# A hybrid encoder layer in float32: later attention pairs read behind a marker, biases one tile ahead, attention and decay started some units later

## The chip, the cores and the metric

The kernel runs on one core of a Trainium2 chip. The metric is the device time of one execution in microseconds (us): 2143.28 is the median of three runs of the kernel before, which lie between 2139.96 and 2145.53. Times inside an execution come from one profiled execution, counted from the start of its span.

A core has engines that run side by side: TensorE (PE; its weight loads are PEld), VectorE (DVE), ScalarE (ACT), GpSimd (POOL) and SyncE (SP). Each works off its own list of instructions strictly in order. An instruction that waits holds up all that stand behind it on its engine. Transfers are started by SP (queue q1 in the profile) and by POOL (queue q0), and all run on the same 16 DMA engines.

## The reference

One encoder layer on a sequence of 1024 tokens with width 1024, all in float32:

```
x = LN1(alpha*x + 0.5*SwiGLU_1(x))
x = LN2(alpha*x + W_out(sig(g_na)*P_na(NA(x)) + sig(g_gla)*P_gla(GLA(x))))
x = LN3(alpha*x + 0.5*SwiGLU_2(x))
```

NA is neighbourhood attention with 8 heads of width 64 on a grid of 16 rows x 64 columns. Each token looks at a window of 8 x 16 tokens; a bias for each offset is added to the scores before the softmax. GLA is gated linear attention with 4 heads, chunked, one scan in each direction, whose decay gates come from a low-rank product. One input projection makes all queries, keys, values and gates of both.

## The kernel before, in words

Every float32 factor is split into a high and a low part (ACT copies the high part, DVE subtracts for the low one), and each product is three matmuls: high x high, high x low, low x high. Three such matmuls of 128 x 512 are one **step**.

The program has stages: the first feed-forward block; the input projection; a stage in which attention runs between dense steps; a GLA stage in the same manner; merging, output projection and norm; the second feed-forward block. The change touches the attention stage and the GLA stage.

**The order on PE is written out by hand.** `run` works through streams of dense steps and adds 0.65 units to a clock for each step. `at(delay, f)` puts a piece of work on a list, and `run` emits it once that clock has passed its time. So a unit is a place in the stream of dense steps, not a time. On the other engines a scheduler places instructions by priority; `hoist()` raises that priority.

**Attention stage.** The dense stream is `tok_major` for the GLA values (8 tiles of 8 steps, lines 871 to 873), then four gate products (lines 122 to 124): 128 steps. Each finished tile of `tok_major` leaves PSUM by an ACT copy into one of two stage buffers (`sl`, line 876) and is stored by SP (`gv<-sl`, line 877). The third copy needs the first store to have landed.

Between these steps run 64 attention tiles, i = 0 to 63. Tile i belongs to head pair i // 16 and to head i % 2 of it; each pair has two blocks of query rows, and each of these four blocks of columns. `na_events` spreads them: event s does the values of tile s-3 (`po`, only for odd tiles), the transposes of tile s-2 (`pt`) and the scores of tile s (`s`). A tile's chain is: scores on PE (lines 1047, 1049), bias added and the minimum taken on DVE (`e`, line 1053), exponential on ACT (line 1055), reciprocal and product on DVE (1057, 1058), three transposes on PE (line 1066), copy on ACT (1069), values on PE (line 1084).

What a head pair needs is read back from DRAM by `qk_pair`: on POOL's queue eight pieces of queries (`q`), four of keys (`k`) and one of the keys' low parts (`kl`); on SP's queue 16 small transfers of values (`vp`, line 1023), whose packets are 512 bytes. All these buffers exist twice. The bias of a tile (`bt`, line 1039) is read by SP when its scores are emitted, at tiles 0, 2, 6, 8, 10, 14 and so on; two tiles share one load and the two middle column blocks too. `bt` has two buffers.

**GLA stage.** `gate_na` streams 8 x 24 dense steps; `gla_decay` of a head begins with two matmuls on the decay ranks (`zs`, line 1172), which need `dlT`, made by ACT and DVE (lines 1150 to 1152) from a small read (`dlr`). `gate_na` frees PSUM with a sigmoid on ACT (line 1296).

Of the kernel before, what the change touches and what calls it, by code (L numbers as in the profile page):

```python
# [8 lines left out]
F32 = mybir.dt.float32  # L9
F32R = mybir.dt.float32r  # L10
BF16 = mybir.dt.bfloat16
U32 = mybir.dt.uint32
AF = mybir.ActivationFunctionType
# [5 lines left out]
P = 128  # L19
# [3 lines left out]
HF = 512  # L23
# [12 lines left out]
NEG = -1.0e30  # L36
HOIST = 100
WARM = 30
GLA_D0 = 6.0
GLA_T0 = 27.0  # L40
GLA_DT = 31.0
GLA_NEXT = 8.5
GLA_OUT = (15.0, 28.8, 28.8, 36.0)
NA_T0 = 13.0
NA_DT = 1.05
NA_GATES = (4, 5, 6, 7)
GLA_GATES = (1, 2, 3)
FIRST = (1, 2, 4, 8)
# [13 lines left out]
COLW = (24, 32, 32, 24)  # L62
BOFF = (0, 288, 288, 672)
# [4 lines left out]
def hybrid_layer(ctx, tc, xT, wg1, wu1, wds1, wd1, wg2, wu2, wds2, wd2, wcol, wnv, wgv, wdl, wgate,  # L68
                 wbr, wout, lnp, bias, dec2, bdec, ng, ident_d, masks_d, ln3, outN):
    nc = tc.nc  # L70
# [4 lines left out]
    def pool(stack, name, bufs=1, space=None):  # L75
        kw = dict(name=name, bufs=bufs)
        if space is not None:
            kw["space"] = space
        if space is not DRAM:
            kw["reuse_waits"] = "tile"  # L80
        return stack.enter_context(tc.tile_pool(**kw))
# [13 lines left out]
    def nm(s):  # L95
        uid[0] += 1
        return f"{s}_{uid[0]}"
# [86 lines left out]
    def at(delay, fn):  # L184
        uid[0] += 1
        pending.append((clock[0] + delay, uid[0], fn))
        pending.sort(key=lambda e: e[:2])

    def run(*streams):
        for st_ in streams:  # L190
            for cost in st_:
                clock[0] += cost
                while pending and pending[0][0] <= clock[0]:
                    pending.pop(0)[2]()
# [6 lines left out]
    def hoist():  # L201
        return tc.high_priority(offset=HOIST)
# [652 lines left out]
    def tok_major(w_d, dst, alloc=None, wq=None):  # L855
        wq = wq or tok_weights(w_d, 4 if alloc is None else 2)
        for i in range(len(wq) // 2, 4):
            raw = wpool.tile([P, D], F32, tag="raw", name=nm("raw"), bufs=2)
            with tc.high_priority(offset=HOIST):
                nc.sync.dma_start(raw, w_d[i])  # L860
                for o in (0, HF):
                    wq.append(alloc())
                    split(raw[:, o:o + HF], *wq[-1])
        for t in range(8):
            h, c = t // 4, (t % 4) * P
            ps = dps()
            for k in range(KD):
                xh, xl = x1[k][h]
                wh, wl = wq[k]
                a, b = xh[:, c:c + P], xl[:, c:c + P]  # L870
                nc.tensor.matmul(ps, a, wh, start=k == 0, stop=False)  # L871
                nc.tensor.matmul(ps, a, wl, start=False, stop=False)
                nc.tensor.matmul(ps, b, wh, start=False, stop=k == KD - 1)  # L873
                yield STEP
            sb = stage()
            nc.scalar.activation(sb, ps, AF.Copy)
            nc.sync.dma_start(dst(t), sb)
# [117 lines left out]
    npool = pool(nap, "npool")  # L995
# [1 line left out]
    grid = lambda t: t.rearrange("p (r c) -> p r c", c=64)  # L997
    pair = {}

    def qk_pair(p):  # L1000
        k2 = [npool.tile([P, S], F32R, tag="k2", name=nm("k2"), bufs=4) for _ in range(2)]
        kl = npool.tile([P, S], F32R, tag="kl", name=nm("kl"), bufs=2)
        vp = npool.tile([P, 16, P], F32, tag="vp", name=nm("vp"), bufs=2)
        q2 = [[None, None], [None, None]]
        pair[p] = (q2, k2, kl, vp)
        load = lambda dst, src: nc.gpsimd.dma_start(dst.bitcast(F32), src)
        for h in range(2):
            hs = slice(h * HF, (h + 1) * HF)
            for hh in range(2):
                a, o = slice(64 * hh, 64 * hh + 64), slice(64 - 64 * hh, 128 - 64 * hh)  # L1010
                t = npool.tile([P, HF], F32R, tag="q2", name=nm("q2"), bufs=8)
                q2[hh][h] = t
                load(t[a], qks[p, 0, a, hs])
                load(t[o], qks[p, 1, a, hs])
                if h == 0:
                    load(k2[hh][a], qks[p, 2, a])
                    load(k2[hh][o], qks[p, 2, a])
            if h == 0:
                load(kl, qks[p, 3])
        for b in range(4):  # L1020
            w = COLW[b]
            for g in range(4):
                nc.sync.dma_start(vp[:4 * w, 4 * b + g, :],  # L1023
                                  vgrid[4 * g:4 * g + 4, COL0[b]:COL0[b] + w, p * P:(p + 1) * P])


    na_e, na_t, na_b, na_o = {}, {}, {}, {}

    def na_idx(i):
        return i // 16, (i // 8) % 2, i % 2, (i // 2) % 4  # L1030

    def na_scores(i):
        p, rb, hh, b = na_idx(i)
        q2, k2, kl, vp = pair[p]
        w, c0 = COLW[b], COL0[b]
        nk = 12 * w
        if hh == 0 and b != 2:
            bt = npool.tile([P, 2, 384], F32, tag="bt", name=nm("bt"), bufs=2)
            nc.sync.dma_start(bt[:, :, :nk], bias[p, rb, :, 2 * BOFF[b]:2 * BOFF[b] + 2 * nk]
                              .rearrange("q (h k) -> q h k", h=2))  # L1040
            na_b[0] = bt
        bt = na_b[0]
        a = slice(64 * hh, 64 * hh + 64)
        ka = (slice(4 * rb, 4 * rb + 12), slice(c0, c0 + w))
        qa = slice(P * b, P * b + P)
        s = aux.tile([P, 384], F32, tag="s", name=nm("s"), bufs=2)
        nc.tensor.matmul(s[:, :nk], q2[hh][rb][:, qa], grid(k2[hh])[:, ka[0], ka[1]],
                         start=True, stop=False)
        nc.tensor.matmul(s[:, :nk], q2[hh][rb][a, qa], grid(kl)[a, ka[0], ka[1]],  # L1049
                         start=False, stop=True)  # L1050
        e = npool.tile([P, 384], F32, tag="e", name=nm("e"), bufs=3)
        sm = npool.tile([P, 4], F32, tag="sm", name=nm("sm"), bufs=4)
        nc.vector.tensor_tensor_reduce(e[:, :nk], s[:, :nk], bt[:, hh, :nk], -1.0,
                                       3.0e38, ALU.add, ALU.min, sm[:, 0:1])
        nc.scalar.activation(e[:, :nk], e[:, :nk], AF.Exp, bias=sm[:, 0:1], scale=-1.0,
                             accum_out=sm[:, 1:2])
        nc.vector.reciprocal(sm[:, 2:3], sm[:, 1:2])
        nc.vector.tensor_scalar(e[:, :nk], e[:, :nk], sm[:, 2:3], None, ALU.mult)
        na_e[i] = e

    def na_transpose(i):
        w = COLW[(i // 2) % 4]
        e = na_e.pop(i)
        pt = aux.tile([P, 384], F32, tag="pt", name=nm("pt"), bufs=1)
        for g in range(3):
            nc.tensor.transpose(pt[:4 * w, g * P:(g + 1) * P], e[:, 4 * w * g:4 * w * (g + 1)],  # L1066
                                ident)
        et = npool.tile([P, 384], F32, tag="et", name=nm("et"), bufs=3)
        nc.scalar.activation(et[:4 * w], pt[:4 * w], AF.Copy)
        na_t[i] = et  # L1070
# [21 lines left out]
    def na_events(s0, s1, t0, t1):  # L1092
        u = (t1 - t0) / (s1 - s0)
        for s in range(s0, s1):
            t = t0 + (s - s0) * u
            if s >= 3:
                at(t, lambda i=s - 3: na_values(i))
            if 2 <= s < 66:
                at(t, lambda i=s - 2: na_transpose(i))
            if s < 64:  # L1100
                at(t, lambda i=s: na_scores(i))

    def gate_gla(j):
        w = load_w(wgate[KD + j], D)
        for h in range(2):
# [3 lines left out]
            nc.scalar.activation(sb, ps, AF.Copy)  # L1109
            nc.sync.dma_start(gts[j, :, h * HF:(h + 1) * HF], sb)  # L1110

    qk_pair(0)
    for p in range(1, 4):
        at(NA_T0 + (16 * p - 13) * NA_DT, lambda p=p: qk_pair(p))
    na_events(0, 67, NA_T0, NA_T0 + 67 * NA_DT)
    run(tok_major(wgv, lambda t: gv[t], wq=wq), *[gate_gla(j) for j in NA_GATES])
    flush()
# [171 lines left out]
    def gate_na(j):  # L1289
        wga = load_w(wgate[j], D)  # L1290
        wb = load_w(wbr[0, j], HF)
        for h in range(2):
            pg = dps()
            yield from mm_steps(pg, wga, x1h[h])
            sb = gp.tile([P, HF], F32, tag="m1", name=nm("m1"), bufs=2)
            nc.scalar.activation(sb, pg, AF.Sigmoid)  # L1296
            py = dps()
            yield from mm_steps(py, wb, [o_na[k][h] for k in range(4)])
            nc.vector.tensor_tensor(sb, sb, py, ALU.mult)
            nc.sync.dma_start(m1s[j, :, h * HF:(h + 1) * HF], sb)  # L1300
# [9 lines left out]

    at(GLA_D0, lambda: gla_decay(0))
    for hd in range(4):
        b = GLA_T0 + GLA_DT * hd
        add = lambda t, f, *a: at(b + t, lambda: f(*a))
# [6 lines left out]
        if hd < 3:  # L1321
            add(GLA_NEXT, gla_decay, hd + 1)
        for i, t in enumerate(GLA_OUT):
            add(t, (gla_out, gla_otrans)[i % 2], hd, i // 2)
# [164 lines left out]
```

## Time and profile before

| what | value |
|---|---|
| median of three runs | 2143.28 us |
| the profiled execution | 2146.0 us, its span 2144.1 us |
| mean granted PE clock | 0.987 |
| PE busy in the span | 2081.7 us (97%) |
| DVE, ACT, POOL busy | 1379.6, 894.3, 156.9 us |
| attention stage, first dense step to the last `po` | 875.1 to 1093.9 us |
| first `zs` of the GLA stage | 1105.1 us |

The span and the profiled execution differ by 1.9 us, which lie outside the span. The profile attributes idle time of an engine to the instruction that released it. Busy time of a group, means and counts are given by line and by tile name with the buffer's number left out, so `bt` is any bias tile.

### The profile page before, as it was taken

What the parts mean: (1) busy time and instruction counts of PE and PEld (TensorE: products, weight loads), DVE (VectorE), ACT (ScalarE), POOL (GpSimd) and SP (SyncE); (2) the same over time, 40 slices, a digit from 0 to 9 for tenths busy, and PEclk for the clock granted to TensorE, in tenths of its full rate; (3) what the DMA queues carried; (4) which work ended last, traced back from release to release, by engine and by line L of the source; (5) the groups of instructions that cost most, each with busy time, mean ns of one, the idle gap of its engine ahead of it and who ended that gap; (6) DMA issues with size and microseconds to landing.
All of it is one profiled execution on the core that took longest, in us unless ns stands there. A gap on an engine that the chain in (4) does not pass through costs nothing.

```text
span 2144.1 us, 26681 instructions
## 1 busy us (share of the span) xinstructions
PE 2081.7 (97%) x9722; PEld 1693.5 (79%) x9722; DVE 1379.6 (64%) x2356; ACT 894.3 (42%) x1500; POOL 156.9 (7%) x204
## 2 busy tenths in 40 slices
PE   9999999999999999679999999999999999999997
PEld 7888888888887788556667888877888888888887
DVE  8667776466678854035447674788876777547647
ACT  6444444312225543135555553445544444322212
POOL 0000000000015021311010000034000000000001
PEclk9999999999999999889999999999999999999999
DMA  4434443496520343646333433622243443386732
GB/s 150 152 133 152 172 148 125 157 334 216 192 88 30 121 164 111 165 125 195 95 107 104 129 109 121 199 96 69 85 173 135 151 174 128 125 295 222 242 108 79
DMA packets 156164, 315.07 MB, mean 147 GB/s; under 512 B 17312, under 2 KB 41632, under 8 KB 156032
## 3 DMA queue, kind: packets, MB, share of 16 engines
q1 hardware_dynamic: 146880, 283.99, 39.4%
q0 software_dynamic: 9152, 29.37, 4.8%
q8 instruction: 77, 1.26, 0.2%
q14 instruction: 55, 0.45, 0.1%
HBM read 216.16 MB, written 97.12 MB: 146 GB/s over the span
## 4 chain that ended last, share of the span: by engine, by line
PE 87%; DVE 6%; SPq 2%; ACT 2%; DMA 1%; issue 1%; POOL 1%; DVEq 0%; ACTq 0%; POOLq 0%
PE d L559 18%; PE d L561 18%; PE d L560 18%; PE d L122 5%; PE d L124 5%; PE d L123 5%; PE d L661 3%; PE d L659 3%; PE d L660 3%; SPq L1023 2%; PE pt L1066 1%; PE po L1084 1%; PE d L871 1%; PE s L1049 1%; PE d L873 1%
## 5 line engine op out<-in xcount | busy, mean ns | idle before, releaser
L131 ACT ACTIVATE wh<-raw 128x512 fp32r<-128x512 f32 (+4 forms) x148 | 111.6, 763 | 194.7 <-PE d L560 86.3
L132 DVE TENSOR_TENSOR wl<-raw,wh 128x512 fp32r<-128x512 f32 (+4 forms) x148 | 125.2, 854 | 101.9 <-ACT wh L131 101.6
L122 PE MATMUL d<-xh,wh 128*128 128x512 f32 x384 | 158.6, 413 | 3.9 <-ACT m L1296 3.5
L681 DVE TENSOR_TENSOR a<-a,d 128x512 f32<-128x512 f32 (+1 forms) x152 | 99.9, 657 | 92.0 <-PE d L561 60.6
L559 PE MATMUL d<-a,wh 128*128 128x512 f32 x384 | 149.8, 390 | 2.4 <-DVE hr L587 1.6
L123 PE MATMUL d<-xl,wh 128*128 128x512 f32 x384 | 150.7, 393 | 1.0 <-POOL xl L412 0.5
L124 PE MATMUL d<-xh,wl 128*128 128x512 f32 x384 | 150.9, 393 | 0.5 <-DVE wl L112 0.5
L561 PE MATMUL d<-xh,wl 128*128 128x512 f32 x384 | 149.5, 389 | 0.5 <-DVE wl L132 0.5
L559 PE MATMUL d<-xh,wh 128*128 128x512 f32 x384 | 149.5, 389 | 0.0
L560 PE MATMUL d<-a,wh 128*128 128x512 f32 x384 | 149.4, 389 | 0.0
L560 PE MATMUL d<-xl,wh 128*128 128x512 f32 x384 | 149.4, 389 | 0.0
L561 PE MATMUL d<-a,wl 128*128 128x512 f32 x384 | 149.4, 389 | 0.0
L559 PE MATMUL d<-hh,hh 128*128 128x512 f32 x384 | 149.4, 389 | 0.0
L560 PE MATMUL d<-hl,hh 128*128 128x512 f32 x384 | 149.4, 389 | 0.0
L561 PE MATMUL d<-hh,hl 128*128 128x512 f32 x384 | 149.4, 389 | 0.0
L131 ACT ACTIVATE hh<-sr 128x512 fp32r<-128x512 f32 x168 | 105.9, 631 | 87.0 <-DVE sr L500 25.1
L659 PE MATMUL d<-hh,wh 128*128 128x512 f32 (+1 forms) x368 | 134.3, 365 | 0.0
L661 PE MATMUL d<-hh,wl 128*128 128x512 f32 (+1 forms) x368 | 133.0, 362 | 0.0
L660 PE MATMUL d<-hl,wh 128*128 128x512 f32 (+1 forms) x368 | 133.0, 361 | 0.0
L112 DVE TENSOR_TENSOR wl<-raw,wh 128x512 fp32r<-128x512 f32 (+1 forms) x77 | 78.0, 1013 | 60.2 <-ACT wh L111 55.4
L132 DVE TENSOR_TENSOR hl<-sr,hh 128x512 fp32r<-128x512 f32 x168 | 114.4, 695 | 1.8 <-ACT hh L131 1.0
L111 ACT ACTIVATE wh<-raw 128x512 fp32r<-128x512 f32 (+1 forms) x77 | 67.6, 878 | 111.2 <-PE d L123 48.9
(330 smaller groups left out, 4909.7 us busy)
## 6 DMA issues: line engine op xcount, KB each, us to landing
raw<-in_wu SPq DMA_DIRECT2D x44, 512.0 KB
raw<-in_wg SPq DMA_DIRECT2D x43, 512.0 KB
ops<-oh SPq DMA_DIRECT2D x84, 256.0 KB
ops<-ol SPq DMA_DIRECT2D x84, 256.0 KB
oh<-ops SPq DMA_DIRECT2D x48, 256.0 KB
ol<-ops SPq DMA_DIRECT2D x48, 256.0 KB
hid<-oh SPq DMA_DIRECT2D x40, 256.0 KB
hid<-ol SPq DMA_DIRECT2D x40, 256.0 KB
```

The lines of the kernel that those rows point to most:

```text
L122: nc.tensor.matmul(ps, a, xh, start=k == 0, stop=False)
L123: nc.tensor.matmul(ps, a, xl, start=False, stop=False)
L124: nc.tensor.matmul(ps, wl[:, k * m:(k + 1) * m], xh, start=False, stop=k == n - 1)
L131: nc.scalar.activation(hi, src, AF.Copy)
L132: nc.vector.tensor_tensor(lo, src, hi.bitcast(F32), ALU.subtract)
L559: nc.tensor.matmul(ps, a, xh, start=first and k == 0, stop=False, **sg)
L560: nc.tensor.matmul(ps, a, xl, start=False, stop=False, **sg)
L561: nc.tensor.matmul(ps, wl[:, k * P:(k + 1) * P], xh, start=False, stop=k == n - 1, **sg)
L659: nc.tensor.matmul(ps, wh, hi, start=k == 0, stop=False)
L660: nc.tensor.matmul(ps, wh, lo, start=False, stop=False)
L661: nc.tensor.matmul(ps, wl, hi, start=False, stop=k == n - 1)
L681: nc.vector.tensor_tensor(a, a, ps, ALU.add)
```

## The change

Five edits:

- `qk_pair` of pairs 1 to 3 gets a marker: one column of the small softmax tile `sm` of the attention tile emitted last. Before any read, POOL copies that column into the first column of each of the seven q, k and kl tiles and into `vp`. The reads write over these cells, so none of the pair's reads, on POOL's queue or on SP's, can begin before DVE has worked on that tile. The call moves from 3 to 5.5 events after the pair before begins (tiles 5, 21 and 37).
- The bias of tile 0 is read ahead of `qk_pair(0)`; every other bias is read when the bias tile before it is taken into use.
- The attention events begin at 20 units instead of 13, and are 0.94 instead of 1.05 units apart.
- In the GLA stage the first decay comes at 8.5 instead of 6 units, the heads at 29.5 + 30.3 per head instead of 27 + 31, and the outputs slightly sooner after them.
- The sigmoid in `gate_na` is hoisted.

```diff
-GLA_D0 = 6.0
-GLA_T0 = 27.0
-GLA_DT = 31.0
+GLA_D0 = 8.5
+GLA_T0 = 29.5
+GLA_DT = 30.3
-GLA_OUT = (15.0, 28.8, 28.8, 36.0)
-NA_T0 = 13.0
-NA_DT = 1.05
+GLA_OUT = (15.0, 28.3, 28.3, 35.5)
+NA_T0 = 20.0
+NA_DT = 0.94
...
-    def qk_pair(p):
+    def qk_pair(p, mark=None):
...
+            for hh in range(2):
+                q2[hh][h] = npool.tile([P, HF], F32R, tag="q2", name=nm("q2"), bufs=8)
+        if mark is not None:
+            m = mark[:, 0:1]
+            for t in (*k2, kl, *q2[0], *q2[1]):
+                nc.gpsimd.tensor_copy(t[:, 0:1], m)
+            nc.gpsimd.tensor_copy(vp[:, :, 0:1], m.unsqueeze(2).to_broadcast([P, 16, 1]))
...
+    def bias_tile(i):
+        p, rb, _, b = na_idx(i)
+        nk = 12 * COLW[b]
+        bt = npool.tile([P, 2, 384], F32, tag="bt", name=nm("bt"), bufs=2)
+        nc.sync.dma_start(bt[:, :, :nk], bias[p, rb, :, 2 * BOFF[b]:2 * BOFF[b] + 2 * nk]
+                          .rearrange("q (h k) -> q h k", h=2))
+        na_b["next"] = bt
...
         if hh == 0 and b != 2:
-            bt = npool.tile([P, 2, 384], F32, tag="bt", name=nm("bt"), bufs=2)
-            nc.sync.dma_start(bt[:, :, :nk], bias[p, rb, :, 2 * BOFF[b]:2 * BOFF[b] + 2 * nk]
-                              .rearrange("q (h k) -> q h k", h=2))
-            na_b[0] = bt
+            na_b[0] = na_b.pop("next")
+            if i < 62:
+                bias_tile(i + (2 if b != 1 else 4))
...
         na_e[i] = e
+        na_mark[0] = sm
...
+    bias_tile(0)
     qk_pair(0)
     for p in range(1, 4):
-        at(NA_T0 + (16 * p - 13) * NA_DT, lambda p=p: qk_pair(p))
+        at(NA_T0 + (16 * p - 10.5) * NA_DT, lambda p=p: qk_pair(p, na_mark[0]))
...
-            nc.scalar.activation(sb, pg, AF.Sigmoid)
+            with hoist():
+                nc.scalar.activation(sb, pg, AF.Sigmoid)
```

**SP at the start of the attention stage.** Before, the list reads (values of pair 0, two stores, biases of tiles 0 and 2, values of pair 1):

```order
L110 DMA raw_8497<-in_wgate 128x1024
L1023 DMA vp_7357<-vscr 96x1x128 x4
L1023 DMA vp_7357<-vscr 128x1x128 x8
L1023 DMA vp_7357<-vscr 96x1x128 x4
L877 DMA gv<-sl_7416 128x512
L877 DMA gv<-sl_7444 128x512
L1039 DMA bt_7463<-in_bias 128x2x288
L1039 DMA bt_7498<-in_bias 128x768
L1023 DMA vp_7519<-vscr 96x1x128 x4
```

With the change (the biases are those of tiles 0, 2, 6, 8, then the values of pair 1, then the biases of tiles 10 and 14):

```order
L1043 DMA bt_7354<-in_bias 128x2x288
L1030 DMA vp_7359<-vscr 96x1x128 x4
...
L877 DMA gv<-sl_7418 128x512
L877 DMA gv<-sl_7446 128x512
L1043 DMA bt_7499<-in_bias 128x768
...
L1043 DMA bt_7676<-in_bias 128x2x288
L1030 DMA vp_7619<-vscr 96x1x128 x4
L1030 DMA vp_7619<-vscr 128x1x128 x8
L1030 DMA vp_7619<-vscr 96x1x128 x4
L877 DMA gv<-sl_7687 128x512
L1043 DMA bt_7727<-in_bias 128x768
L1043 DMA bt_7778<-in_bias 128x2x288
```

The first bias has moved ahead of the 16 value reads of pair 0. The first stores and the bias of tile 2 are still behind them. The bias of tile 10 stands behind the 16 value reads of pair 1, which now wait for POOL's copies. In the same way the biases of tiles 26 and 42 stand directly behind the value reads of pairs 2 and 3.

**ACT at the start of the attention stage.** Before (`sl` is the copy of a finished `tok_major` tile, `e` the exponential of tiles 0 and 1):

```order
L876 ACTIVATE sl_7416<-d_7391 128x512
L876 ACTIVATE sl_7444<-d_7419 128x512
L1055 ACT_TABLE_LOAD
L1055 ACTIVATE e_7468,sm_7469<-e_7468,sm_7469 128x288
L1055 ACTIVATE e_7480,sm_7481<-e_7480,sm_7481 128x288
L876 ACTIVATE sl_7509<-d_7447 128x512
```

With the change:

```order
L876 ACTIVATE sl_7418<-d_7393 128x512
L876 ACTIVATE sl_7446<-d_7421 128x512
L876 ACTIVATE sl_7474<-d_7449 128x512
L1069 ACT_TABLE_LOAD
L1069 ACTIVATE e_7504,sm_7505<-e_7504,sm_7505 128x288
L876 ACTIVATE sl_7513<-d_7477 128x512
```

The third copy, which needs the first store's buffer back, now stands ahead of the first exponential. On PE the first scores follow 31 dense steps instead of 21.

**ACT at the start of the GLA stage**, with the change (`m` is the sigmoid's tile; before, all four `dlT` copies stood ahead of the table load):

```order
L1166 ACTIVATE dlT<-dlr_9266 32x512
L1313 ACT_TABLE_LOAD
L1313 ACTIVATE m_2179_9313<-d_9288 128x512
L1167 ACTIVATE dlT<-dlr_9266 32x512
L1166 ACTIVATE dlT<-dlr_9271 32x512
L1167 ACTIVATE dlT<-dlr_9271 32x512
```

The sigmoid with its table load has moved between the copies that `zs` needs. On PE the first `zs` follows 142 dense steps of the two stages instead of 138.

More of the change, by code (lines that the diff above doesn't have):

```diff
@@ L1007, in qk_pair @@
         for h in range(2):
+            for hh in range(2):
[5 more added lines that the diff above has]
+            nc.gpsimd.tensor_copy(vp[:, :, 0:1], m.unsqueeze(2).to_broadcast([P, 16, 1]))
+        for h in range(2):
             hs = slice(h * HF, (h + 1) * HF)
@@ L1010, in qk_pair @@
                 a, o = slice(64 * hh, 64 * hh + 64), slice(64 - 64 * hh, 128 - 64 * hh)
-                t = npool.tile([P, HF], F32R, tag="q2", name=nm("q2"), bufs=8)
-                q2[hh][h] = t
+                t = q2[hh][h]
                 load(t[a], qks[p, 0, a, hs])
@@ L1024, in qk_pair @@
                                   vgrid[4 * g:4 * g + 4, COL0[b]:COL0[b] + w, p * P:(p + 1) * P])
-    na_e, na_t, na_b, na_o = {}, {}, {}, {}
+    na_e, na_t, na_b, na_o, na_mark = {}, {}, {}, {}, {}
     def na_idx(i):
         return i // 16, (i // 8) % 2, i % 2, (i // 2) % 4
+    def bias_tile(i):
[5 more added lines that the diff above has]
+        na_b["next"] = bt
     def na_scores(i):
```

## The prediction

> **What bounds the kernel now.** I read the page's first line, then the list of waits between 840 and 1130 us for PE and DVE (columns: time in total, times, longest), since PE is busy 97% of the span and the change touches only this part.
>
> ```profile
> span 2144.1 us, 26681 instructions
> ...
> PE pt L1066 <- DVE e L1058: 22.0, 1, 22.0
> PE s L1049 <- DMA kl<-qks: 5.4, 1, 5.4
> PE zs L1172 <- DVE dlT L1152: 4.2, 2, 3.5
> ...
> DVE e L1053 <- DMA bt<-in_bias: 44.8, 2, 43.6
> ```
>
> PE stands still twice at the first attention tiles, 5.4 us for the keys' low part and 22.0 us at the first transpose. The second is the bias: DVE waited 43.6 us for it in one go. The view by stretches (length, then busy time of PE, PEld, DVE, ACT, POOL, then granted clock) shows what follows a stall:
>
> ```profile
> 896.00:901.00 5.00, 4.81 (x11) 2.91 (x10) 0.00 (x0) 0.00 (x0) 3.22 (x7) 0.55 0.85 197
> 923.00:932.00 9.00, 9.00 (x35) 6.00 (x34) 2.48 (x9) 2.54 (x7) 0.00 (x0) 0.54 0.39 112
> 1107.00:1113.00 6.00, 6.00 (x17) 4.71 (x16) 1.88 (x2) 4.76 (x7) 0.35 (x1) 0.57 0.30 94
> ```
>
> After each stall PE runs at little over half clock: 4.81 x 0.45 = 2.2, 9.0 x 0.46 = 4.1 and 6.0 x 0.43 = 2.6 us lost, 3.0 us a stall on average. The Trainium skill (TensorE: Matmul & The Clock Gate, Part 1: The HAM clock gate) puts the slow time at some 3.4 us of sustained work; the trace shows 5 to 9 us, and by the page each stall below would cost 1.7 us instead of 3.0.
>
> So the first tiles lose 5.4 + 22.0 + 2.2 + 4.1 = **33.7 us**, which is all this part of the change can give back. Why the bias is late is in SP's own list (start, duration, instruction):
>
> ```profile
> 877.82 37.31 SPq L1023 DMA_DIRECT2D vp<-vscr  x16
> 915.24 0.88 SPq L877 DMA_DIRECT2D gv<-sl  x2
> 916.21 0.94 SPq L1039 DMA_DIRECT2D bt<-in_bias  x2
> ...
> 968.76 10.73 SPq L1023 DMA_DIRECT2D vp<-vscr  x16
> ```
>
> The bias stands behind 16 value reads, which hold SP 37.31 us here and 10.73 us in the third group. What differs is POOL's queue q0, in the views of the transfers (packets, MB, share of the DMA engines) of 880.4 to 893.4, of 910 to 912.5 and of 971 to 979 us:
>
> ```profile
> q0 software_dynamic: 831, 2.61, 95.1%
> q1 hardware_dynamic: 334, 0.23, 7.7%
> ...
> q0 software_dynamic: 39, 0.10, 12.4%
> ...
> q1 hardware_dynamic: 1362, 0.71, 31.4%
> ```
>
> While POOL's reads run, SP's queue moves 0.23 MB in 13 us; without them 0.71 MB in 8 us. POOL's last reads run out by 912.5 us, and SP is free at 915.2. SP's transfers do not share, they wait until POOL's are through. This row decides the case.
>
> **The change part by part.** The sum goes against the profiled execution's 2146.0 us; the median of the runs is 2.7 us lower.
>
> *First tiles.* The rows of PE, ACT and DVE that I use:
>
> ```profile
> 875.12 0.39 PE L871 MATMUL d<-wh,xh 128*128 128x512 f32 x1
> ...
> 875.80 0.39 PE L871 MATMUL d<-wh,xh 128*128 128x512 f32 x1
> ...
> 889.40 0.29 PE L1047 MATMUL s<-k,q 128*128 128x288 f32 x1
> 895.12 0.60 PE L1049 MATMUL s<-kl,q 64*128 64x288 f32 x1 [5.42 <-DMA kl<-qks]
> ...
> 922.80 0.87 PE L1066 MATMUL pt<-ident,e 128*96 128x128 f32 x3 [21.99 <-DVE e L1058]
> ...
> 886.20 0.60 ACT L876 ACTIVATE sl<-d 128x512 f32<-128x512 f32 x1 [4.84 <-PE d L873]
> 886.82 1.28 ACT L1055 ACT_TABLE_LOAD   x1
> 921.52 0.54 ACT L1055 ACTIVATE e<-e,sm 128x288 f32<-128x288 f32 x1 [33.42 <-DVE sm L1053]
> ...
> 921.02 0.46 DVE L1053 CUSTOM_DVE_ANT_0 e<-s,bt 128x288 f32<-128x288 f32 x1 [43.60 <-DMA bt<-in_bias]
> ```
>
> A dense step takes 0.68 us. The first scores stand 10 steps later, at 889.4 + 6.8 = 896.2 us, after the 895.1 at which the keys have landed: the 5.4 us are gone. The first bias, now ahead of the values, has 0.29 MB and lands before that or about then. But PE reaches the first transpose 3 steps and two score pairs of 0.63 us on, at 899.5, and there ACT is late: its third copy stands ahead of the first exponential and needs the first `gv` store to have landed, which SP still starts behind the 16 value reads. Pair 0's reads on POOL end at about 893.4: the transfers of 876 to 916 us list, for two pairs,
>
> ```profile
> q<-qks POOLq DMA_DIRECT2D x16, 128.0 KB, 9.0
> k<-qks POOLq DMA_DIRECT2D x8, 256.0 KB, 10.0
> kl<-qks POOLq DMA_DIRECT2D x2, 512.0 KB, 11.6
> ```
>
> or 2.6 MB a pair, and the row of 880.4 to 893.4 has 2.61. The last value read leaves SP some time later: bounds are 3.2 us (before: from about 912 to 915.2) and 10.7 (nothing issued ahead). I take 8, as the bias is ahead. The store goes at 901.9 and takes 4 us (bounds 2 and the 4.8 us from the bias's issue at 916.21 to DVE at 921.02). So ACT goes on at 905.9, and with copy 0.60, table load 1.28 and the 1.28 from the exponential's start to the transpose (921.52 to 922.80) PE goes on at 909.0. Stall **9.5 us** (bounds 2.7 and 13.0), with the clock 12.5. The bias of tile 2 hides in it.
>
> *The marker.* Eight small POOL copies a pair. The nearest rows:
>
> ```profile
> 1088.73 0.10 POOL L1136 MEMSET rmask<- 128x8 f32 x1
> ...
> 1087.52 0.95 POOL L1135 MEMSET rmask<- 128x1024 f32 x1 [79.66 <-PE s L1047]
> ```
>
> So 0.8 to 7.6 us for eight; they are one column wide, I take 1.6. The copies cost no busy engine anything. What they release is the point: POOL's 2.62 MB and SP's 16 value reads now start together, after tiles 5, 21 and 37, and behind the value reads SP holds the bias of tiles 10, 26 and 42, five tiles on. In the profile the second and third groups of values started when POOL's reads were through. Now it is as at 877.8 us:
>
> ```profile
> 877.65 1.06 POOL L1006 DMA_DIRECT2D q<-qks  x2
> ```
>
> From this issue to the end of that pair's reads at 893.4 are 15.7 us. Then 6 us until SP has issued the last value read (bounds 3.2 and 10.7; no bias is ahead here), 0.9 for the store and the bias (0.88 for two in the row), 4.8 to landing: **27.4 us** after the copies. With 1.6 for the copies and 1.8 from DVE's start to the transpose (921.02 to 922.80), the transposes of tile 10 can run 30.8 us after DVE has done tile 5. PE gets there earlier. Between lie 10 steps, six score pairs, six groups of transposes and four of values, whose lengths I take from
>
> ```profile
> 1084.29 0.88 PE L1084 MATMUL po<-et,vp 128*64 128x128 f32 x12
> 1085.10 0.55 PE L1066 MATMUL pt<-ident,e 128*128 128x128 f32 x3
> 1085.40 0.38 PE L1047 MATMUL s<-k,q 128*128 128x288 f32 x1
> ...
> 1086.03 0.50 PE L122 MATMUL d<-xh,wh 128*128 128x512 f32 x1
> ```
>
> by their starts: 0.81 + 0.1 for values, 0.30 transposes, 0.63 to 0.72 scores, 0.68 + 0.1 a step after scores: 3.6 + 1.8 + 4.0 + 7.5 = 16.9, less 0.6 for DVE's pass, 16.3 us of cover. Stall 30.8 - 16.3 = **14.5 us**, with the clock 17.5, and the same for pairs 2 and 3, whose lists differ little: 52.5. Bounds: with no hold-up at all SP needs 10.73 + 0.9 + 4.8 = 16.4 us and the stall is 3.5; with the mean of 37.31 and 10.73 for the 16 reads (half of POOL's traffic) it is 24.0 + 5.7 = 29.7 and 16.8.
>
> *Spacing.* 0.94 against 1.05 units changes which steps lie between, not their number; PE does the same work. Cost nothing.
>
> *GLA.* `zs` comes four steps later, 2.7 us, but the hoisted sigmoid with its table load (1.28 + 0.60) now stands between the copies it waits for. Of 4.2 us, 3.4 stay, and the clock loss too. The sigmoids themselves are awaited by PE in
>
> ```profile
> PE d L122 <- ACT m L1296: 3.5, 3, 1.2
> ```
>
> of which hoisting may take all or, with more table loads, nothing; I take 1.5. Together **-2.3 us**, between -10.3 (4.2, 2.6 and 3.5 all gone) and +4 (the decay chain late by two table loads and reaching its transposes).
>
> Sum: -33.7 + 12.5 + 52.5 - 2.3 = +29.0, or 2175.0 for the profiled execution; against the median, 2143.3 + 29.0 = 2172.3.
>
> **The rivals.**
>
> *Both queues get their turn (faster).* The place is the DMA engines while POOL reads pairs 1 to 3. If SP's small packets are served alongside, the 16 reads need about the 10.73 us of the quiet case, the first store lands in time, and the three stalls are 3.5 us: -33.7 + 3 x (3.5 + 2) - 2.3 = -19.5, some 2124; with a landing in under 2 us nothing stalls and it is 2107. It decides once SP needs under some 14 us for the 16 reads. For it speaks the 10.73 us of the third group, whose first reads still met POOL's last; against it 7.7% to 95.1% above. The Trainium skill says this would be the rule (DMA: Bandwidth & Descriptors, Queues, rings and completion order): each DMA engine goes round its queues packet by packet. The transfers of 880.4 to 893.4 us do not agree, 334 packets against 831 with SP's list full. By the page it is the faster rival that holds.
>
> *Part of the hold-up (no change).* If POOL's reads take 10 us, because no weights are read beside them, and SP has issued more ahead, the bias lands after 20 us: stalls of 7.1 + 3, and 6 + 3 at the first transpose: -33.7 + 9 + 30.3 - 2.3 = +3.3, some 2147.
>
> *The marker does not hold the reads back.* Then the pairs collide as before. POOL's copies stand ahead of the reads in its list and SP's value reads wait for POOL, so I give this next to nothing.
>
> **How the numbers follow.** Forecast 2172 with its own range 2154 to 2188: 0.60. Turns: 0.23. Part: 0.13, of which 0.04 falls under, 0.08 within and 0.01 above. Worse than 2188 (the gate weights that SP reads ahead of pair 2's values add to it): 0.04. A measurement of this kernel can tell about 0.3%, 6.4 us, from no change, so: faster 0.27, same 0.08, slower 0.65. The range takes in the turns' middle and the upper bound of the reads: 2118 to 2188.
>
> **What would show it.** In the profile after: no wait for kl at the first scores, a wait of about 9 us at the first transpose with ACT behind it; three waits of PE at transposes, some 14 us each and 45 us apart, put down to the exponentials' tile and on DVE to the bias; 16 value reads that hold SP over 18 us each time; half clock after each. It would be wrong if these groups take 11 to 13 us beside POOL's reads, if the scheduler's place of the bias leaves more lead than five tiles, or if the first store lands before 900 us.

## The result, and the profile after

The changed kernel takes 2175.43 us (median of 4 runs, 2172.99 to 2177.49) against 2143.97 us of the kernel before on the same occasions. The ratio is 1.0149, with a 95% interval of 1.0131 to 1.0167: slower by 31.5 us. The forecast was 2172 us, 29 us slower.

The changed kernel's list of waits between 840 and 1180 us (total, times, longest), which answers to the first list of the prediction. PE's lines first, then what DVE and ACT waited for:

```profile
span 2173.7 us, 26722 instructions
...
PE pt L1081 <- DVE sm L1071: 45.2, 3, 15.9
PE pt L1081 <- DVE e L1072: 11.7, 1, 11.7
...
DVE e L1067 <- DMA bt<-in_bias: 50.4, 3, 17.6
...
ACT sl L876 <- DMA gv<-sl: 21.4, 1, 21.4
```

The wait for `kl` and the one of 22.0 us are gone. In their place stand one of 11.7 us at the first transpose, behind which ACT stood 21.4 us for the first `gv` store, and three of 15.1 us on average, behind which DVE stood for the bias. The rows of POOL, SP, DVE and PE in the timeline (start, duration; idle before in brackets) of the first of the three, and PE's rows of the other two:

```profile
923.75 0.31 POOL L1013 CAST k<-sm 128x1 fp32r<-128x1 f32 x2 [32.50 <-DVE sm L1067]
...
924.59 0.21 POOL L1014 COPY vp<-sm 128x16 f32<-128x16 f32 x1
...
924.83 22.15 SPq L1030 DMA_DIRECT2D vp<-vscr  x16
...
947.60 0.96 SPq L1043 DMA_DIRECT2D bt<-in_bias  x2
...
952.12 0.56 DVE L1067 CUSTOM_DVE_ANT_0 e<-s,bt 128x384 f32<-128x384 f32 x1 [15.98 <-DMA bt<-in_bias]
...
954.22 0.87 PE L1081 MATMUL pt<-ident,e 128*128 128x128 f32 x3 [14.27 <-DVE sm L1071]
...
1013.94 0.87 PE L1081 MATMUL pt<-ident,e 128*128 128x128 f32 x3 [15.90 <-DVE sm L1071]
...
1071.95 0.88 PE L1081 MATMUL pt<-ident,e 128*128 128x128 f32 x3 [15.07 <-DVE sm L1071]
```

POOL's copies end at 924.80 us, the 16 value reads hold SP from 924.83 to 946.98, the bias of tile 10 is issued behind them and DVE has it at 952.12, 27.3 us after the copies. The stretches behind the four waits (length, PE's busy time; after the engines comes the granted clock) show half clock each time:

```profile
911.49:918.00 6.51, 6.51 (x17) 4.43 (x18) 1.91 (x7) 2.03 (x6) 0.00 (x0) 0.50 0.14 52
954.22:962.40 8.18, 8.18 (x23) 5.42 (x25) 2.63 (x9) 2.40 (x6) 0.00 (x0) 0.50 0.14 36
1013.00:1020.40 7.40, 6.46 (x17) 4.48 (x18) 2.90 (x11) 3.13 (x10) 0.00 (x0) 0.50 0.09 35
1071.95:1078.40 6.45, 6.45 (x17) 4.44 (x18) 2.85 (x9) 3.30 (x8) 0.00 (x0) 0.50 0.14 47
```

Half of PE's busy time there is lost: 3.3 us behind the first wait, and 4.1 + 3.2 + 3.2 = 10.5 behind the three. The account of the attention stage is then -33.7 + 11.7 + 3.3 + 45.2 + 10.5 = +37.0 us. The stage's own length, from its first dense step to its last values, can be read directly: in the changed kernel

```profile
875.20 0.39 PE L871 MATMUL d<-wh,xh 128*128 128x512 f32 x1
...
1128.05 0.88 PE L1099 MATMUL po<-et,vp 96*64 96x128 f32 x12
```

and in the kernel before (its first dense step, at 875.12, stands in the prediction)

```profile
1092.99 0.88 PE L1084 MATMUL po<-et,vp 96*64 96x128 f32 x12
```

That is 252.85 against 217.87 us, +35.0; 2.0 us of the account are not resolved. What lies behind the last values has become shorter, 1045.65 instead of 1051.11 us. So the two spans differ by 35.0 - 5.5 = 29.5 us. The profiled execution of the kernel before took 2146.0 us, 2 us more than the median of its runs, so some of the 5.5 us may belong to that one execution. Whether they come from the change's GLA part is a question for the runs below.

### The profile page after: what moved, and what is told of

The parts are those of the page before. It is cut to its first block, busy times and chain, and to the rows that moved or that the text cites. A ratio compares the mean times of both kernels' runs of the same rounds, so it can differ in the third digit from the quotient of the medians.

```text
span 2173.7 us, 26722 instructions
## 1 busy us (share of the span) xinstructions
PE 2084.4 (96%) x9722; PEld 1695.7 (78%) x9722; DVE 1377.6 (63%) x2356; ACT 901.7 (41%) x1506; POOL 161.3 (7%) x228
```

## The experiments

The theory to be tested is the prediction's: the marker releases POOL's reads and SP's 16 value reads together, the value reads are slow beside POOL's, and the bias that stands behind them on SP comes late. The rivals are that the later and closer tiles make the waits, that the value reads are slow by themselves, and, within the theory, two accounts of the slowness: that SP's transfers wait until POOL's are through, as the prediction put it, or that the queues take turns.

**The marker left out.** The edit, on the changed kernel:

```diff
-        at(NA_T0 + (16 * p - 10.5) * NA_DT, lambda p=p: qk_pair(p, na_mark[0]))
+        at(NA_T0 + (16 * p - 10.5) * NA_DT, lambda p=p: qk_pair(p))
```

> The changed kernel without the marker's copies; everything else stays. Theory (the three waits after tiles 5, 21 and 37 come from the value reads that the marker releases together with POOL's reads and that stand ahead of the bias): the three waits (45.2 us in the changed kernel, and about 10 us at half clock behind them) are gone, but the reads of two pairs meet the first tiles again and the first gv store stands behind value reads that hold SP some 37 us, so the wait at the first transpose grows from 11.7 to about 22 us. Time about 2132 us (2126 to 2142). Rival (the later start and the closer spacing of the tiles make the waits): they stay, 2165 us or more.

Measured: 2142.67 us, ratio to the kernel before 0.9996 (0.9986 to 1.0006). PE's largest waits in this run:

```profile
PE pt L1081 <- DVE e L1072: 24.8, 1, 24.8
PE pt L1081 <- ACT et L1084: 7.0, 1, 7.0
```

SP's first value reads in its timeline, and the row of ACT ahead of the second wait, which ends at 992.60 us:

```profile
879.10 38.33 SPq L1030 DMA_DIRECT2D vp<-vscr  x16
...
991.11 1.06 ACT L111 ACTIVATE wh<-raw 128x1024 fp32r<-128x1024 f32 x1 [7.84 <-DMA raw<-in_wgate]
```

The three waits are gone, so the marker makes them and not the spacing. The reads of two pairs meet again at the start, SP is held for 38.33 us, and the first wait grows to 24.8 us, 2.8 more than I expected. The wait of 7.0 us is not at the first tiles and I had not expected it: ACT stood 7.84 us for a read of gate weights, which SP issues behind the value reads of pair 2, at 982.19 us, and the copy of the transposes stands behind it on ACT. Together these are 9.8 of the 10.7 us by which the time lies over the expected 2132.

**The bias three reads ahead.** The marker stays; only the place of the bias on SP changes (four buffers; a list hands out the next tile):

```diff
-        bt = npool.tile([P, 2, 384], F32, tag="bt", name=nm("bt"), bufs=2)
+        bt = npool.tile([P, 2, 384], F32, tag="bt", name=nm("bt"), bufs=4)
...
-            if i < 62:
-                bias_tile(i + (2 if b != 1 else 4))
+            if na_todo:
+                bias_tile(na_todo.pop(0))
...
-    bias_tile(0)
+    for _ in range(3):
+        bias_tile(na_todo.pop(0))
```

> The changed kernel with four bias buffers and the bias read three reads ahead, so that the biases of tiles 10 and 14 stand ahead of the value reads on SP; marker and reads stay as they are. Theory: the value reads hold SP 22 us as before, but no tile waits for its bias, the three waits and the half clock behind them (about 55 us) are gone, the first one of 11.7 us stays or grows by a microsecond or two, since more bias is read beside pair 0: about 2121 us (2114 to 2130). Rival (what is late is not the bias but all that POOL's reads hold up, so that the waits move to the values): waits of over 8 us each at the values' matmuls, 2150 us or more.

Measured: 2124.04 us, ratio 0.9907 (0.9892 to 0.9921). PE's largest wait between 880 and 1095 us, at the first tiles:

```profile
PE pt L1081 <- DVE e L1072: 14.1, 2, 13.3
```

SP's reads of pair 1:

```profile
923.90 22.43 SPq L1030 DMA_DIRECT2D vp<-vscr  x16
```

The stretch from 925 to 1075 us, with its granted clock behind the engines:

```profile
925.00:1075.00 150.00, 147.83 (x898) 101.97 (x898) 71.33 (x246) 80.20 (x199) 26.22 (x63) 1.00 0.56 153
```

The value reads hold SP as long as in the changed kernel, and nothing waits for them: PE is busy for 147.83 of 150 us at full clock. The three waits are the bias behind the value reads. The waits did not move to the values.

**The value reads on POOL's queue.**

```diff
-                nc.sync.dma_start(vp[:4 * w, 4 * b + g, :],
+                nc.gpsimd.dma_start(vp[:4 * w, 4 * b + g, :],
```

> The changed kernel with the 16 value reads of each pair on POOL's queue, behind its own reads; SP's list holds biases and stores alone. Theory (SP's transfers get little while POOL's run, whatever stands in SP's list): POOL's reads are now 3.5 MB and take some 20 us, the bias of tile 10 still moves slowly beside them and lands near their end; three waits of 4 to 9 us stay, and the first transpose still waits for the first gv store, 5 to 12 us: 2140 to 2160 us. Rival (order alone: the bias is late only because 16 value reads stand ahead of it): bias and store land within 5 us of their issue, no waits: about 2105 us.

Measured: 2160.76 us, ratio 1.0079 (1.0064 to 1.0094). The time is slightly over the expected one, but for another reason than either theory had. PE's waits in this run:

```profile
PE po L1099 <- DMA vp<-vscr: 32.5, 15, 4.2
PE pt L1081 <- DVE e L1072: 3.0, 2, 2.0
```

and the first and the last of pair 0's 16 value reads in POOL's timeline:

```profile
890.40 0.73 POOL L1030 DMA_DIRECT2D vp<-vscr  x1 [1.45 <-issue]
...
931.47 0.66 POOL L1030 DMA_DIRECT2D vp<-vscr  x1 [2.75 <-issue]
```

The three waits for the bias are gone and the first transpose hardly waits: SP's biases and stores land in time while POOL reads. Now the values are late: POOL needs 41.7 us for the 16 reads, 2.6 us each, though one is at most 0.73 us of its time. What it waits for between them is not shown. So the waits fell away although POOL's list was longer than before; this speaks against the account that SP's transfers wait for POOL's end. The transfers of 880.2 to 890 us in this run (packets, MB, share of the DMA engines) say it directly:

```profile
q0 software_dynamic: 532, 1.68, 69.1%
q1 hardware_dynamic: 529, 0.91, 32.8%
```

Beside them those of the changed kernel from 928 to 936 us, and last, with POOL silent, from 940.5 to 946.5 us:

```profile
q0 software_dynamic: 524, 1.68, 92.3%
q1 hardware_dynamic: 299, 0.15, 10.8%
...
q1 hardware_dynamic: 924, 0.46, 27.9%
```

With biases and stores in its list, SP's queue moves as many packets as POOL's, and 0.91 MB in 9.8 us. With value reads in it, it moves 299 packets of 0.5 KB against POOL's 524 of 3.2 KB, or 37 in a microsecond; with POOL silent 924 in 6 us, 154 in a microsecond. So SP's queue is served beside POOL's all the time, and the account that it waits until POOL's is through is wrong. By my reading the value reads are slow because their packets are small: each waits for packets six times as long.

That reading does not cover the end of POOL's reads. From 938 to 940 us of the changed kernel the two queues fill little more than a quarter of the DMA engines' time, and SP's still moves only 25 packets in a microsecond:

```profile
q0 software_dynamic: 57, 0.17, 23.4%
q1 hardware_dynamic: 50, 0.02, 4.3%
```

SP's queue is fast only once POOL's last packets are gone. What holds it back until then is not shown.

**Half the bytes in as many packets.**

```diff
-                nc.sync.dma_start(vp[:4 * w, 4 * b + g, :],
-                                  vgrid[4 * g:4 * g + 4, COL0[b]:COL0[b] + w, p * P:(p + 1) * P])
+                nc.sync.dma_start(vp[:4 * w, 4 * b + g, 0:64],
+                                  vgrid[4 * g:4 * g + 4, COL0[b]:COL0[b] + w, p * P:p * P + 64])
...
-                                 vp[:4 * w, 4 * b + rb + g, 64 * hh:64 * hh + 64],
+                                 vp[:4 * w, 4 * b + rb + g, 0:64],
```

> The changed kernel with value reads that bring the first 64 of the pair's 128 columns alone (both heads use these, so the second head's values are left out): as many packets, half the bytes. If the queues take turns by packet, 16 reads still hold SP 18 to 22 us beside POOL's reads, and the three waits stay 11 to 16 us each: 2163 to 2176 us. If what counts is bytes: 10 to 13 us, waits of 0 to 5 us, 2125 to 2145 us.

Measured: 2161.74 us, ratio 1.0078 (1.0058 to 1.0098). SP's reads of pair 1:

```profile
919.33 20.18 SPq L1030 DMA_DIRECT2D vp<-vscr  x16
```

PE's largest waits:

```profile
PE pt L1081 <- DVE sm L1071: 38.5, 3, 13.7
```

The transfers of 923 to 931 us:

```profile
q0 software_dynamic: 533, 1.70, 93.8%
q1 hardware_dynamic: 436, 0.11, 9.3%
```

With half the bytes SP is held 20.18 us instead of 22.15, and the three waits are 12.8 us each instead of 15.1. So the bytes count for little. What counts is the number of packets or that of the transfers, 16 in both kernels; no run parts these two. Strict turns by packet would give SP's queue as many packets as POOL's: 436 against 533 is nearer to that than 299 against 524, and neither reaches it.

**The value reads of pairs 1 to 3 six tiles later,** in a function of their own and with their own mark, the bias again behind them:

```diff
+        at(NA_T0 + (16 * p - 4.5) * NA_DT, lambda p=p: v_pair(p, na_mark[0]))
```

> The changed kernel with the value reads of pairs 1 to 3 marked and issued six tiles after the pair's other reads, when POOL's reads are through; bias one tile ahead as in the change, and again behind the value reads. Theory (the value reads hold SP for 22 us only because POOL reads beside them): alone they hold SP about 11 us, the bias behind them lands about 17 us after the mark, against a cover of 16.3, so the three waits are 0 to 3 us each, the first one of 11.7 stays: 2120 to 2134 us. Rival (16 value reads hold SP as long by themselves): 22 us again, three waits of 12 to 16 us, 2165 us or more.

Measured: 2140.41 us, ratio 0.9978 (0.9967 to 0.9989). SP's reads of pair 1:

```profile
939.90 10.84 SPq L1035 DMA_DIRECT2D vp<-vscr  x16
```

PE's waits between 880 and 1095 us:

```profile
PE pt L1086 <- DVE e L1077: 15.8, 2, 11.8
PE pt L1086 <- DVE sm L1076: 7.9, 3, 3.2
```

The stretches behind the waits that end at 957.68, 1005.06 and 1051.33 us, with the granted clock:

```profile
957.68:965.00 7.32, 7.32 (x35) 5.03 (x35) 3.67 (x10) 4.33 (x8) 0.00 (x0) 0.77 0.14 40
1005.06:1012.00 6.94, 6.94 (x25) 4.72 (x27) 1.85 (x7) 2.25 (x6) 0.00 (x0) 0.64 0.18 55
1051.33:1060.00 8.67, 8.67 (x35) 5.54 (x36) 2.87 (x10) 2.88 (x7) 0.00 (x0) 0.63 0.13 34
```

The same 16 reads hold SP 10.84 us once POOL is silent, so they are slow beside POOL's reads and not by themselves. The first line of the waits is the one at the first tiles (11.8) and that of the second marked pair (4.1); the second line holds those of the other two (3.2 each) and one of 1.6 in between. So the three waits shrink from 15.1 to 3.5 us on average, a little over the 0 to 3 that I expected. The time is 6 us over the expected range, since I had left out that such waits also cost clock afterwards: 0.23 x 7.32 = 1.7, 0.36 x 6.94 = 2.5 and 0.37 x 8.67 = 3.2 us.

**The bias on ACT's queue.**

```diff
-        nc.sync.dma_start(bt[:, :, :nk], bias[p, rb, :, 2 * BOFF[b]:2 * BOFF[b] + 2 * nk]
+        nc.scalar.dma_start(bt[:, :, :nk], bias[p, rb, :, 2 * BOFF[b]:2 * BOFF[b] + 2 * nk]
```

> The changed kernel with the biases read from ACT's queue instead of SP's; the value reads stay on SP beside POOL's reads. As the prediction put it (SP's transfers wait until POOL's are through, and so would ACT's): the bias of tiles 10, 26 and 42 lands some 20 us after the copies, three waits of about 7 us stay, 2148 us or more. Rival, after the run with the values on POOL (the queues take turns packet by packet, and a bias packet is as long as POOL's): the bias lands within 9 us, the three waits are under 2 us each, only the first one of 11.7 us stays: 2118 to 2130 us.

Measured: 2166.16 us, ratio 1.0100 (1.0085 to 1.0115). This run doesn't decide what it was made for. ACT's rows around the first of the waits:

```profile
944.99 0.38 ACTq L1043 DMA_DIRECT2D bt<-in_bias  x1
945.41 0.60 ACT L131 ACTIVATE a<-po 128x512 fp32r<-128x512 f32 x1 [14.40 <-DMA vp<-vscr]
```

ACT stood for 14.4 us, which the profile puts down to the value reads; by the order of the rows it stood at the issue of a bias, and with it the exponentials behind. A wait for the bias's landing seems to have been replaced by one at its issue. What binds that issue to the value reads was not tried.

**The first store ahead of the values.** On the kernel with the bias three ahead, pair 0's value reads come later, so that the first `gv` store stands ahead of them on SP and the second after eight of them:

```diff
+    at(13.0, lambda: v_pair(0))
```

> The kernel with the bias three reads ahead, and pair 0's value reads issued later, so that the first gv store stands ahead of them on SP and the second after eight of them. Theory (the wait at the first transpose is ACT's third copy waiting for the first gv store, which stands behind 16 value reads): the store lands in 4 to 8 us although POOL is reading, ACT is not held, the wait of 13.3 us and some 3 us at half clock are gone; up to 4 us may come back where the second store or the last values are late. From 2124 to about 2109 us (2106 to 2114). Rival (SP's transfers get next to nothing until POOL's reads are through, whatever their order): the store lands after 893 us as before, 4 to 8 us of the wait stay, 2116 us or more.

Measured: 2113.75 us, ratio 0.9853 (0.9837 to 0.9870). PE's largest wait between 880 and 1095 us, and ACT's waits for the stores:

```profile
903.91 0.50 PE L1086 MATMUL pt<-ident,e 128*96 128x128 f32 x3 [2.63 <-DVE e L1077]
...
ACT sl L876 <- DMA gv<-sl: 14.0, 2, 9.9
```

The stretch of 900 to 915 us, with its granted clock:

```profile
900.00:915.00 15.00, 12.37 (x58) 8.34 (x57) 4.73 (x18) 6.11 (x16) 1.11 (x9) 0.77 0.39 118
```

The wait of 13.3 us at the first transpose is down to 0.2, so the store behind the value reads made it. ACT still waits 9.9 us for the first store, which goes at 880.06 and lands at about 895.4, not in 4 to 8 us; ahead of it on SP stand the first three biases. ACT goes on at 895.4, and PE reaches the first transpose at 898.6. The 2.6 us are at the second transpose: its exponential stands behind ACT's next copy, which waits 4.1 us for the second store. The lost clock (0.23 x 15 = 3.5 us) stays.

**Reads spread further.** One bias instead of three ahead of the first store, and pair 0's values a column block at a time:

```diff
-    for _ in range(3):
-        bias_tile(na_todo.pop(0))
+    bias_tile(na_todo.pop(0))
+    for t in (10.0, 12.5):
+        at(t, lambda: bias_tile(na_todo.pop(0)))
...
-    at(13.0, lambda: v_pair(0))
+    for b, t in enumerate((9.5, 14.0, 16.0, 17.0)):
+        at(t, lambda b=b: v_pair(0, None, [b]))
```

> The run with the store first, but with one bias read instead of three ahead of the first store on SP (the next two come behind it), and pair 0's value reads issued a column block at a time between the stores. There the first store landed 15 us after its issue, behind 0.99 MB of bias, and the second behind eight value reads; PE waited 3.4 us at transposes, 1.7 us at values, and ran at half clock for some 7 us. If the first store is late because of what SP has ahead of it, it lands in 5 to 9 us, the 2.6 us wait and the half clock are gone: 2106 to 2111 us. If POOL's reads set it, no change: 2112 to 2116 us.

Measured: 2114.04 us, ratio 0.9860 (0.9842 to 0.9878): no gain. ACT's third copy:

```profile
900.56 0.60 ACT L876 ACTIVATE sl<-d 128x512 f32<-128x512 f32 x1 [12.89 <-DMA gv<-sl]
```

The first store did not land sooner: it goes at 882.26 us, with one bias and three value reads ahead of it, and lands at about 900.5, after 18.3 us instead of 15.3. The number of biases ahead of it does not explain that, and what sets the landing of a store beside POOL's reads stays open.

**The GLA part alone, and everything but it.** The four GLA constants and the hoisted sigmoid, once put into the kernel before, and once taken out of the run with the store first.

```diff
-GLA_D0 = 6.0
-GLA_T0 = 27.0
-GLA_DT = 31.0
+GLA_D0 = 8.5
+GLA_T0 = 29.5
+GLA_DT = 30.3
...
-GLA_OUT = (15.0, 28.8, 28.8, 36.0)
+GLA_OUT = (15.0, 28.3, 28.3, 35.5)
...
-            nc.scalar.activation(sb, pg, AF.Sigmoid)
+            with hoist():
+                nc.scalar.activation(sb, pg, AF.Sigmoid)
```

> The kernel before with the change's GLA part alone (the four GLA constants and the hoisted sigmoid); attention as before. The prediction's term is -2.3 us: 2141 us. From the changed kernel's trace (zs waits 1.9 instead of 4.2, no half clock there, no waits for the sigmoids, a new wait of 1.4 for the decayed keys): -7 us, 2137 us. If the GLA gain came only because the attention ahead of it was shifted: 2144 us.

> The run with the store first, with the GLA part as it was before the change (four constants, sigmoid not hoisted). The prediction's term is -2.3 us, so this should be 2.3 us slower than the store first run: 2116 us. By the profiles, in which the time behind the last values is 5 to 6 us shorter with the change's GLA part: 2119 to 2120 us. If the GLA part is worth nothing: 2114 us.

Measured: alone 2141.98 us, ratio 0.9993 (0.9983 to 1.0002), or -1.4 us; without it 2111.71 us, ratio 0.9853 (0.9838 to 0.9869), the same ratio as with it. PE's waits for the decays in the run with the GLA part alone:

```profile
PE zs L1172 <- ACT dlT L1151: 2.3, 1, 2.3
PE zs L1172 <- DVE dlT L1152: 1.0, 1, 1.0
```

and the stretch around them:

```profile
1100.00:1116.00 16.00, 12.73 (x48) 9.78 (x47) 3.27 (x4) 11.67 (x14) 0.56 (x1) 0.89 0.54 144
```

The same in the run with the store first and the old GLA part, where PE waits for the sigmoids again (3.5 us), and its stretch around them:

```profile
PE zs L1197 <- DVE dlT L1177: 1.8, 2, 1.0
...
1075.00:1090.00 15.00, 13.15 (x57) 10.24 (x56) 6.03 (x6) 13.09 (x16) 0.56 (x1) 1.00 0.43 128
```

With the GLA part alone the wait for `zs` is 3.3 us instead of 4.2 and the clock still falls (0.89); with the old GLA part behind a changed attention stage it is 1.8 and the clock stays at 1.00. From the start of the last values to the end of the span it is 1051.1 us in the kernel before, 1047.1 with the GLA part alone, 1044.6 with the changed attention and the old GLA part, and 1045.1 with both. So either part alone shortens what lies behind attention in these profiles, and behind a changed attention stage the GLA part adds nothing. What there sets the wait for `zs` was not tried.

The best of these runs, 2111.7 and 2113.8 us, which their intervals do not part, are faster than both kernels: 1.5% under the kernel before and 2.9% under the changed one.

## Why the prediction was right, point by point

**What is given back.** The 5.4 us for `kl` and the 22.0 us for the first bias are gone, as forecast, and with them the half clock behind them.

**The first transpose.** Forecast 9.5 us with 3 of half clock, measured 11.7 and 3.3. The mechanism was the right one (ACT's third copy, the first store, 16 value reads), and the run with the store first shows it: 13.3 falls to 0.2, with 2.6 at the next. The term was small by 2.2 us: SP was through with the values at 903.8 us, where the prediction had the store at 901.9, and ACT went on at 908.3 and not at 905.9.

**The marker's waits.** Forecast 27.4 us from the copies to the bias, measured 27.3; forecast 14.5 us of wait, measured 14.27, 15.90 and 15.07; forecast 3.0 us of half clock each, measured 4.1, 3.2 and 3.2. Together 55.7 us against 52.5. The waits end 59.7 and 58.0 us apart, not 45, which is about what lies between two of them without the wait itself (43.8 and 42.9). The copies took 1.05 us of POOL where I put 1.6, and cost no busy engine anything.

**The account of the hold-up was wrong, though its length was right.** The prediction said that SP's transfers "do not share, they wait until POOL's are through", from 334 packets against 831. They do share, though SP's queue is fast only once POOL's is empty. I read that row by its bytes and by the share of the DMA engines, 7.7% against 95.1%; its packets already showed SP's queue at two of POOL's five. In the changed kernel the ratio is 299 to 524, and with biases and stores 529 to 532. The 16 reads are 8 x 128 + 8 x 96 = 1,792 packets (a row of 128 values each). As an estimate, at the 37 a microsecond of 928 to 936 us 15.7 us pass 580 of them, and the other 1,212 need 7.9 us at 154 a microsecond: 23.6 us, against 22.15 for SP's issues. My 15.7 + 6 = 21.7 us came out near that because most packets were left over when POOL's reads ended. That the length was right is luck in part, since the 6 us came from a wrong account.

**The rival of turns.** Its premise, that SP's packets are served alongside, held; its price did not. It gave the reads 10.73 us, and they took 22.15: beside POOL's packets of 3.2 KB a queue of 0.5 KB packets moved 37 in a microsecond instead of 154. The rule of the Trainium skill (DMA: Bandwidth & Descriptors, Queues, rings and completion order) is that each DMA engine goes round its queues packet by packet. The 529 against 532 packets agree with it, 299 against 524 less well; and a packet of that page holds some 9 to 17 descriptors (orders to move one piece), which no run here sets against a packet of the profile. In any case it is a rule of packets and not of bytes, and so it does not lead to the faster time, as the prediction took it to.

**Spacing.** Forecast nothing. No run moved the spacing alone; with the marker out and the spacing in, the three waits were gone, so it makes none of them.

**GLA.** Forecast -2.3 us; alone -1.4 us, within an interval that holds both that and nothing, and behind the changed attention stage it adds nothing. The prediction said that 3.4 of the 4.2 us at `zs` and the clock loss stay; in the changed kernel the waits there are 1.9 us and the granted clock from 1130 to 1150 us is 1.00. This comes with the changed attention stage ahead, by the run with the old GLA part, and the prediction had no term for it.

So the total came out near because the attention terms were small by 3.7 us (31.3 against 35.0) and the stage behind it gained 3.2 us more than forecast. The terms of the stalls had the right cause and nearly the right size; that these two errors cancel is luck.

## What to carry to other kernels

In these runs, reads of many small packets that started together with reads of long ones were slow for as long as the long ones lasted; their bytes did not show it, half the bytes hardly helped. Put what is needed soon (a bias, a store that frees a buffer) ahead of such a list on its queue, or start the list when the other queue is silent: here these two turned 1.5% slower into 1.5% faster. When a marker holds reads back until a place in the program, look at everything that is queued behind the reads, since all of it is held back too. Price a wait with the clock behind it: here waits of 3.2 to 4.1 us cost another 1.7 to 3.2.

## What the runs showed of the hardware

Two queues that run together did not share the DMA engines by bytes. Beside POOL's packets of 3.2 KB, SP's queue moved 37 packets a microsecond of 0.5 KB (299 against 524), 55 of 0.25 KB (436 against 533) and 54 of 1.7 KB on average (529 against 532); with POOL silent it moved 154 of 0.5 KB. Halving the bytes of the small packets shortened their 16 reads by 2.0 us of 22.15.

A value read of 96 to 128 packets that takes 0.68 us of SP's list in a quiet time (10.84 us for 16) took 2.6 us of POOL's (41.7 us for 16), at most 0.73 us of it on POOL and the rest put down to the issue itself.

Half clock lasted some 6.5 to 8.2 us after stalls of 11.7 to 15.9 us. The Trainium skill (TensorE: Matmul & The Clock Gate, Part 1: The HAM clock gate) lets the clock come back after some 3.4 us of sustained work; the measured times are longer. The clock also fell after waits of 3.2 us (to 0.77 and 0.63 over the next 7 to 9 us), and not after one of 1.6 us (1.00 from 986.45 to 993 us of the run with the values six tiles later).
